# Eight value tiles of differential attention made in pairs with the gates, and two leading tiles in the last projection

## The chip, the cores and the metric

One core of a Trainium2 chip. The metric is the device time of one execution in microseconds (us); lower is better. Times before and after are medians of several runs, and one execution of each kernel was profiled.

## The reference

A two-layer trunk for 512 latent tokens and 128 context tokens (640 rows, width 2048), all in float32. Both layers: RMSNorm with a shift and a scale computed from the conditioning vector, one wide input projection whose columns are split between mixers, an output projection, and a gated residual. The second ("odd") layer, which the change is about, has differential attention (C, four heads) and grouped-query attention (D):

```
cq, ck, cv, cg, dq, dk, dv, dg = split_cols(h @ w_in, ODD_SPLIT)
...
cv = cv.reshape(b, t, C_HEADS, C_V_DIM).transpose(0, 2, 1, 3)     # 4 heads, 256 columns each
...
new = (ck, cv, k_d, v_d)                     # of the context tokens; these are outputs
cv_all = jnp.concatenate([ctx[1], cv], axis=2)      # latent tokens: cached rows, then their own
o1 = attend(cq[:, 0][:, :, None], ck_all[:, 0], cv_all)[:, :, 0]
o2 = attend(cq[:, 1][:, :, None], ck_all[:, 1], cv_all)[:, :, 0]
o_c = rms_norm(o1 - lam * o2, c_on) * (1.0 - lam_init)
y_c = o_c.transpose(0, 2, 1, 3).reshape(b, t, C_W) * jax.nn.silu(cg)
y_d = merge_heads(attend(q_d, dk_all, dv_all)) * jax.nn.silu(dg)
return jnp.concatenate([y_c, y_d], axis=-1) @ w_out, new
```

`cv`, the values of C, are 1024 columns of the projection: eight tiles of 128, two for each head. `cg` and `dg` are the gates, eight tiles each.

## The kernel before

Activations stay transposed: a tile is 128 columns of a projection on the partitions, by 640 tokens. Every float32 operand is split into a rounded part and a rest (`split`: a copy on ACT for `hi`, a subtraction on DVE for `lo`), and a product is three matmuls: hi x hi, hi x lo, lo x hi. A tile needs 16 rows of K, each in two halves of 320 tokens: 16 x 2 x 3 = 192 matmuls of 128x320, into two PSUM tiles `pa` and `pb`.

There are two ways to make tiles.

- **Singles** (`run_tiles`): a tile at a time, in four quarters (`proj_q`, four rows of K in each half: 24 + 24 matmuls). Weights come as `raw` by SP's queue, quarters ahead, and are split into `wh`, `wl` (four buffers each). After every quarter `slot` advances other work: `prep` holds what follows a tile (`q_gen`, `k_gen`, `v_gen`), `attn` holds attention (`pair_gen` for D, `diff_gen` for C, one step a call), and `fill` is a generator that is called at a given rate. With `steps` above 1 attention gets more than one step a quarter.
- **Pairs** (`run_pairs`, called at the end of `project`): two tiles by two halves of the tokens by two halves of K in seven products of 24 matmuls (`pq`) instead of eight, with sums of weights and of inputs made on DVE beside them. Results arrive as four halves of 320 tokens by `done`.

A projection begins with leading tiles, made side by side as the rows of `h` become ready; the third of them takes the PSUM tile `Sp`, which shares its two banks with attention's scores `S`.

The order of the stages around the change is:

1. Front of the odd layer (the `project` call at line 1430, jobs `FRONT`): 14 of the 16 gate tiles, three leading, three single, eight in four pairs. `gate_out` makes silu's two instructions for each half and stores the tile in `gdram`.
2. The odd run (`run_tiles` at line 1484) with 38 tiles: 12 for D, six for each C head (`q0 q1 k0 k1 v0 v1`), and at last the gates 4 and 5 (`very_late_gate`). `k_gen` norms and rotates a key in four quarters and calls `drain(attn)` before it overwrites keys; `v_gen` stages a value tile, transposes it to rows, splits it, and after the second value tile of a head appends the head's attention. The fill of this run, `fill1`, makes the last four column blocks of the second layer's modulation on DVE (`ada_on_dve`): for each block 32 loads `adaw` of 128 KB by SP's queue into three buffers, two multiply-adds of 128x256 on DVE for each (lines 211 and 213), then a sum over partitions on PE (`T<-acc,ones`, line 219), a copy on ACT and a transpose. A block is 33 calls; the rate is `FILL1 = 1.0` a quarter after the first 16 quarters (`FILL1_FROM`).
3. The last projection (`project_out(1, ...)`, order of K quarters 0, 2, 3, 1): `y1_maker(k)` loads row tile k of the mixers' output from `ydram` (`yin`) and splits it into `h`. At k = 12 it finishes `fill1` and attention, closes the pool `odd`, opens `fin`, and starts the `forms` for the pairs. Three tiles lead, three are single, ten are in five pairs.

```
    brisk = {len(jobs), len(jobs) + 1}
    ...
    run_tiles(jobs, I["od_w_in"][0], None, fill1, FILL1, fill_from=FILL1_FROM,
              steps=lambda i: 1.5 if i in brisk else 1.0)
    drain(prep)
    drain(attn)

    def y1_maker(k):
        if k == 12:
            for _ in fill1:
                pass
            drain(attn)
```

Tile (the layer under the kernel) puts each engine's instructions into a fixed order at build time and sets the semaphores; engines work through their lists in that order, and so does SP with its DMA issues.

Of the kernel before, what the change touches and what calls it, by code (L numbers as in the profile page):

```python
# [11 lines left out]
F32 = mybir.dt.float32  # L12
F32R = mybir.dt.float32r
# [7 lines left out]
P = 128  # L21
# [32 lines left out]
def trunk_kernel(ctx: ExitStack, tc: tile.TileContext, I: dict, O: dict):  # L54
# [520 lines left out]
                                   op0=ALU.add, op1=ALU.mult)  # L575


    def k_gen(ap, pp, tag, src, gain, new_out):
        raw = ap.tile([P, 2, P], F32, tag="ctxk", name="ctxk", bufs=1)
        nc.sync.dma_start(raw, src.rearrange("(c p) d -> p c d", p=P))  # L580
        x = stage(ap, pp)
        yield
        ss = small.tile([P, 5], F32, tag="ss", name="ss")
        kg = ap.tile([P, 5, P], F32, tag="rp", name="kg", bufs=3)
        junk = ap.tile([P, P * st["sets"]], F32, tag="junk", name="junk", bufs=1)[:, 0:P]
        for sample in (True, False):
            t = to_rows(cols_of(x), sample)
            for i, b in enumerate(range(4) if sample else (4,)):
                A.activation(junk, t[:, i * P:(i + 1) * P], AF.Square, accum_out=ss[:, b:b + 1])
            if sample:  # L590
                V.tensor_mul(kg[:, 0:4, :], t.rearrange("p (b f) -> p b f", b=4),
                             gain[:, None, :].to_broadcast([P, 4, P]))
            else:
                V.tensor_mul(kg[:, 4, :], t, gain)
        r = small.tile([P, 5], F32, tag="r", name="r")
        V.tensor_scalar(ss, ss, 1.0 / P, EPS, ALU.mult, ALU.add)
        G.tensor_tensor(r, ss, half[:, 0:5], op=ALU.pow)
        V.tensor_mul(kg, kg, r[:, :, None].to_broadcast([P, 5, P]))
# [12 lines left out]
        yield  # L611
        drain(attn)
        hi, lo = (ap.tile([P, 896], F32R, tag=tag + t, name=tag + t) for t in "hl")
        st[tag] = (hi, lo)
        t = psT()
        for c in range(2):
            PE.transpose(t[:, c * P:(c + 1) * P], raw[:, c, :], ident)
        split(hi[:, 0:CTX], lo[:, 0:CTX], t[:, 0:CTX])
        t = to_rows(lambda b: m1[:, b, :], True)
        split(hi[:, CTX:CTX + NS], lo[:, CTX:CTX + NS], t)  # L620
        t = to_rows(lambda b: kg[:, b, :], False)
        split(hi[:, CTX + NS:CTX + NT], lo[:, CTX + NS:CTX + NT], t)


    def q_gen(ap, pp, tag, gain, then=None, wait=True):
# [46 lines left out]
    def v_gen(ap, pp, src, new_out, w=P, j=0, then=None):  # L672
        x = stage(ap, pp)
        yield
        if j == 0:
            drain(attn)
            st["v"] = tuple(ap.tile([P, 7, w], F32R, tag=t, name=t) for t in ("vh", "vl"))
            ctx_v(ap, src, *st["v"], w)
        hi, lo = st["v"]
        cols = slice(j * P, (j + 1) * P)  # L680
        t = to_rows(cols_of(x), True)
        split(hi[:, 2:6, cols], lo[:, 2:6, cols], t.rearrange("p (b f) -> p b f", b=4))
# [3 lines left out]
        split(hi[:, 6, cols], lo[:, 6, cols], vp)  # L686
        nc.gpsimd.dma_start(new_out, vp)
        if then:
            attn.append(then())
# [141 lines left out]
    xdram, hdram, gdram = ([dram.tile([P, NT], F32, name=f"{n}{k}") for k in range(KT)] for n in ("xd", "hd", "gd"))  # L831

    y = [None] * KT
    st = {"sets": 1}
# [89 lines left out]
        open_pool("even")  # L924


    def k_job(tag, src, gain, new_out):
        return lambda pp: k_gen(pools["cur"], pp, tag, src, gains[gain], new_out)

    def v_job(src, new_out, *a):  # L930
        return lambda pp: v_gen(pools["cur"], pp, src, new_out, *a)
# [179 lines left out]
    def form_of(i):  # L1111
        return lambda j: (T[j][:, 0, i * HALF:(i + 1) * HALF], T[j][:, 1, i * HALF:(i + 1) * HALF])

    def project(w, cols, n0, maker, job, begin, part, done, tail, **kw):

        go_on = run_tiles([(cols[n], job(n)) for n in range(3)], w, maker, **{"order": (0, 2, 1, 3), **kw})


        quarters = [(cols[n], qd) for n in range(3, n0) for qd in range(4)]
# [10 lines left out]
        for n in range(3, n0):  # L1130
            pp, t = new_pp((n - 3) % 2), 4 * (n - 3)
# [270 lines left out]

    half_done, outs = set(), {}

    def front_job(n):
        def f(pp):
            put = gate_out(n)
# [11 lines left out]
    def front_tail(name):  # L1419

        if name == "P6":
# [8 lines left out]
    project(I["od_w_in"][0], [(OD["cg"] + i * P) if i < 8 else OD["dg"] + (i - 8) * P for i in FRONT], N_FRONT, h1_maker,  # L1430
            front_job, front_begin, None, front_done, front_tail, by_half=True)
    nc.sync.dma_start(tables, I["k_tables"])
    close("mid")
# [28 lines left out]
    for n in range(4):  # L1462
# [3 lines left out]
        jobs.append((OD["dq"] + (h + 1) * P, q_job("q1", "d_q_norm", then if n % 2 else None)))  # L1466
        if n % 2 == 0:
            jobs.append((OD["dk"] + kv * P, k_job(f"k{kv}", I["cache_d_k"][0, 0, kv], "d_k_norm", O["new_d_k"][0, 0, kv])))
            jobs.append((OD["dv"] + kv * P, v_job(I["cache_d_v"][0, 0, kv], O["new_d_v"][0, 0, kv], P, 0, then)))
    for h in range(4):  # L1470
        for m in range(2):
            jobs.append((OD["cq"] + (m * 4 + h) * P, q_job(f"q{m}", "c_q_norm")))
        for m in range(2):
            jobs.append((OD["ck"] + (m * 4 + h) * P,
                         k_job(f"k{m}", I["cache_c_k"][0, 0, m, h], "c_k_norm", O["new_c_k"][0, 0, m, h])))
        for j in range(2):
            jobs.append((OD["cv"] + h * 256 + j * P,
                         v_job(I["cache_c_v"][0, 0, h], O["new_c_v"][0, 0, h][:, j * P:(j + 1) * P], 256, j,
                               diff_then(h) if j else None)))
# [4 lines left out]
    run_tiles(jobs, I["od_w_in"][0], None, fill1, FILL1, fill_from=FILL1_FROM,  # L1484
              steps=lambda i: 1.5 if i in brisk else 1.0)
    drain(prep)
    drain(attn)


    def y1_maker(k):  # L1490
# [95 lines left out]
```

## Time and profile before

| | |
|---|---|
| median of 3 runs | 2317.5 us (2316.15 to 2321.3) |
| profiled execution | 2318.59 us, span 2316.8 us |
| mean granted TensorE clock | 0.997 |
| PE matmul busy | 2272.1 us (98%) |
| DVE, ACT, POOL busy | 1635.5, 969.7, 175.6 us |
| memory read, written | 301.93 MB, 38.28 MB |

The span is the time from the first to the last instruction; what lies around it is the difference to the execution's own time. PE is TensorE's matmul row, PEld its weight loads, DVE VectorE, ACT ScalarE, POOL GpSimd, SP the engine that issues most DMAs. In the groups the numbers are the sum of busy time, the mean of one instruction in ns, and the idle time of the engine ahead of them with what ended it. Matmuls are pipelined and their recorded durations overlap.

### The profile page before, as it was taken

To read this page: it belongs to the slowest core of one execution; us is meant where nothing else is said; L and a number is where in the kernel's file an instruction comes from. 1 tells how busy PE (TensorE), PEld (TensorE's weight loads), DVE (VectorE), ACT (ScalarE), POOL (GpSimd) and SP (SyncE) were. 2 spreads that over 40 slices of the span, in tenths; PEclk is the share of its full clock that TensorE was granted. 3 is DMA by queue.
4 is the path that set the end of the run, shared out by engine and by line. 5 is a ranking of instruction groups with operands and counts; after the bars stand their busy time and mean duration, and the time that the engine had idled before them with its cause. 6 is when DMAs were issued, how large, how long until landed. Compare 5 with 4: busy or idle time off the path is not lost.

```text
span 2316.8 us, 41604 instructions
## 1 busy us (share of the span) xinstructions
PE 2272.1 (98%) x15892; PEld 2197.3 (95%) x15892; DVE 1635.5 (71%) x3308; ACT 969.7 (42%) x2007; POOL 175.6 (8%) x243
## 2 busy tenths in 40 slices
PE   7999999999999999999999999999999999999999
PEld 5699999999999999999999999999999999999999
DVE  4559886786866663988887658659657658557576
ACT  4335442433422222544644445555453444434343
POOL 2111000000000000000100000000001010100101
PEclk9999999999999999999999999999999999999999
DMA  9874545445455543844773433224315233318532
GB/s 364 330 260 130 154 124 163 144 122 165 121 180 160 152 139 114 283 140 127 242 223 107 135 102 97 63 81 131 97 52 153 66 92 113 92 60 281 176 119 70
DMA packets 388456, 342.94 MB, mean 148 GB/s; under 512 B 19298, under 2 KB 327024, under 8 KB 387744
## 3 DMA queue, kind: packets, MB, share of 16 engines
q1 hardware_dynamic: 376000, 294.35, 41.9%
q0 software_dynamic: 11536, 43.77, 5.0%
q8 instruction: 125, 2.05, 0.4%
q10 hardware_dynamic: 720, 2.16, 0.3%
q14 instruction: 75, 0.61, 0.1%
HBM read 301.93 MB, written 38.28 MB: 147 GB/s over the span
## 4 chain that ended last, share of the span: by engine, by line
PE 86%; DVE 4%; ACT 3%; DMA 3%; issue 2%; POOL 1%; SPq 0%; ACTq 0%; POOLq 0%; DVEq 0%
PE pa L276 9%; PE pb L277 9%; PE pb L276 9%; PE pa L277 9%; PE pb L278 9%; PE pa L278 9%; PE pq L535 5%; PE pq L537 5%; PE pq L536 5%; PE T L715 2%; PE T L178 1%; PE S L727 1%; PE S L729 1%; PE S L728 1%; DMA yin<-yd 1%
## 5 line engine op out<-in xcount | busy, mean ns | idle before, releaser
L241 ACT ACTIVATE wh<-raw 128x512 fp32r<-128x512 f32 (+1 forms) x466 | 288.4, 619 | 723.8 <-PE pb L277 615.4
L276 PE MATMUL pa<-h,wh 128*128 128x320 f32 x1632 | 519.2, 319 | 4.8 <-ACT h L908 2.5
L242 DVE TENSOR_TENSOR wl<-raw,wh 128x512 fp32r<-128x512 f32 (+1 forms) x466 | 313.8, 674 | 296.3 <-ACT wh L241 260.9
L277 PE MATMUL pa<-h,wh 128*128 128x320 f32 x1632 | 508.3, 312 | 2.8 <-DVE h L242 2.7
L278 PE MATMUL pa<-h,wl 128*128 128x320 f32 x1632 | 506.9, 311 | 0.0
L278 PE MATMUL pb<-h,wl 128*128 128x320 f32 x1632 | 505.5, 310 | 0.0
L276 PE MATMUL pb<-h,wh 128*128 128x320 f32 x1632 | 505.2, 310 | 0.0
L277 PE MATMUL pb<-h,wh 128*128 128x320 f32 x1632 | 505.0, 309 | 0.0
L213 DVE SCALAR_TENSOR_TENSOR acc<-adaw,sT,acc 128x512 f32<-128x512 f32 (+1 forms) x600 | 358.3, 636 | 14.0 <-DMA adaw<-in_ada_w 13.7
L276 PEld LDWEIGHTS pa<-h,wh 128*128 128x128 f32 x1632 | 307.9, 189 | 18.2 <-issue 9.3
L277 PEld LDWEIGHTS pa<-h,wh 128*128 128x128 f32 x1632 | 308.4, 189 | 7.3 <-DVE h L242 4.5
L278 PEld LDWEIGHTS pa<-h,wl 128*128 128x128 f32 x1632 | 307.9, 189 | 3.3 <-issue 3.3
L278 PEld LDWEIGHTS pb<-h,wl 128*128 128x128 f32 x1632 | 306.6, 188 | 2.1 <-issue 2.1
L276 PEld LDWEIGHTS pb<-h,wh 128*128 128x128 f32 x1632 | 306.7, 188 | 0.0
L277 PEld LDWEIGHTS pb<-h,wh 128*128 128x128 f32 x1632 | 306.5, 188 | 0.1
L535 PE MATMUL pq<-h,wh 128*128 128x320 f32 x480 | 149.7, 312 | 0.4 <-DVE xr L1099 0.2
L536 PE MATMUL pq<-h,wh 128*128 128x320 f32 x480 | 148.4, 309 | 0.0
L537 PE MATMUL pq<-h,wl 128*128 128x320 f32 x480 | 148.0, 309 | 0.0
L701 ACT ACTIVATE p<-S,nm,rq 128x768 f32<-128x768 f32 (+3 forms) x120 | 101.2, 843 | 101.4 <-DVE nm L696 67.1
L535 PE MATMUL pq<-T,wh 128*128 128x320 f32 x360 | 111.2, 309 | 0.0
L536 PE MATMUL pq<-T,wh 128*128 128x320 f32 x360 | 111.2, 309 | 0.0
L537 PE MATMUL pq<-T,wl 128*128 128x320 f32 x360 | 111.2, 309 | 0.0
(326 smaller groups left out, 3699.8 us busy)
## 6 DMA issues: line engine op xcount, KB each, us to landing
adaw<-in_ada_w SPq DMA_DIRECT2D x192, 256.0 KB, 3.0
raw<-in_ev_w_in SPq DMA_DIRECT2D x184, 256.0 KB, 3.0
raw<-in_od_w_in SPq DMA_DIRECT2D x184, 256.0 KB, 2.9
ada<-in_ada_w SPq DMA_DIRECT2D x14, 2048.0 KB, 10.5
adaw<-in_ada_w SPq DMA_DIRECT2D x128, 128.0 KB, 2.2
yd<-y POOLq DMA_DIRECT2D x32, 320.0 KB, 3.0
yin<-yd SPq DMA_DIRECT2D x32, 320.0 KB, 4.4
w<-yd SPq DMA_DIRECT2D x32, 320.0 KB, 4.1
```

Of the source, the lines that this page charges most:

```text
L178: PE.matmul(acc[32 * g:32 * g + 32, 0:wd], sT[:, kt, :], w[:, kt % m, :], start=(i < 4), stop=(i >= KT - 4), tile_position=(0, 32 * g))
L213: V.scalar_tensor_tensor(out=a, in0=w, scalar=sT[:, kt, c:c + 1], in1=a, op0=ALU.mult, op1=ALU.add)
L241: A.activation(hi, x, AF.Copy)
L242: V.tensor_sub(lo, x, hi)
L276: PE.matmul(ps, wh[:, i, :], hi[:, sl], start=(j == js[0] if alone else (pos == 0 and j == 0)), stop=False)
L277: PE.matmul(ps, wh[:, i, :], lo[:, sl], start=False, stop=False)
L278: PE.matmul(ps, wl[:, i, :], hi[:, sl], start=False, stop=(j == js[1] - 1 if alone else (pos == 3 and j == 3)))
L535: PE.matmul(ps, wh[:, j, :], hi, start=(h == 0 and j == 0), stop=False)
L536: PE.matmul(ps, wh[:, j, :], lo, start=False, stop=False)
L537: PE.matmul(ps, wl[:, j, :], hi, start=False, stop=(h == 1 and j == 3))
L701: A.activation(p[:, 0:n], s, AF.Exp, scale=rsc, bias=nm, accum_out=l)
L715: PE.transpose(t[:, i * P:(i + 1) * P], p, ident)
```

## The change

The eight value tiles of C leave the odd run and join the front as four more pairs behind the gates'. `value_out` copies each half to SBUF; when a tile is whole, `value_rows` transposes it to rows of tokens, stores it in `vdram` (128x640), and writes the context part to the output. In the odd run the first key tile of a C head (`k0`) now also loads the head's two value tiles back (`vx`, in the buffers `stg`), and splits them with the cached values; the second key tile (`k1`) appends the head's attention. The odd run has 30 tiles instead of 38; from tile 13 on attention gets 1.1 steps a quarter, and 1.5 in the two last gates as before. The last projection has two leading tiles instead of three, hence four single ones; attention is no longer drained at the end of the odd run but runs on beside the first two units of the leading tiles, which leave `S` free. So `y1_maker` takes its first eight rows into the buffers `rp` and `stg` instead of `P`, which attention still uses.

```diff
-    def k_gen(ap, pp, tag, src, gain, new_out):
+    def k_gen(ap, pp, tag, src, gain, new_out, vals=None, then=None):
+        vx = []
+        def v_in(j):
+            vx.append(ap.tile([P, 5, P], F32, tag="stg", name="vx", bufs=2))
+            nc.sync.dma_start(vx[j].rearrange("p b f -> p (b f)"), vals[1][j])
...
         x = stage(ap, pp)
+        if vals:
+            v_in(0)
         yield
...
+        if vals:
+            v_in(1)
...
+        if vals:
+            yield
+            hi, lo = st["v"] = tuple(ap.tile([P, 7, 2 * P], F32R, tag=t, name=t) for t in ("vh", "vl"))
+            ctx_v(ap, vals[0], hi, lo, 2 * P)
+            for j in range(2):
+                cols = slice(j * P, (j + 1) * P)
+                split(hi[:, 2:7, cols], lo[:, 2:7, cols], vx[j])
+        if then:
+            attn.append(then())
...
-    def project(w, cols, n0, maker, job, begin, part, done, tail, **kw):
+    def project(w, cols, n0, maker, job, begin, part, done, tail, n_lead=3, **kw):
...
+    def value_rows(n, t):
+        yield
+        r = pools["cur"].tile([P, 5, P], F32, tag="xr", name="vr", bufs=3)
+        A.copy(r[:, 0:4, :], to_rows(cols_of(st[t]), True).rearrange("p (b f) -> p b f", b=4))
+        A.copy(r[:, 4, :], to_rows(cols_of(st[t]), False))
+        nc.gpsimd.dma_start(vdram[n], r.rearrange("p b f -> p (b f)"))
+        nc.gpsimd.dma_start(O["new_c_v"][0, 0, n // 2][:, n % 2 * P:(n % 2 + 1) * P], r[:, 4, :])
+
+    def value_out(n):
+        def put(t, sl, src):
+            A.copy(st[t][:, sl], src)
+            if (n, "v") in half_done:
+                prep.append(value_rows(n, t))
+            half_done.add((n, "v"))
+        return put
...
-            outs[t] = gate_out(N_FRONT + 2 * p + t)
+            n = N_FRONT + 2 * p + t
+            outs[t] = gate_out(n) if n < len(FRONT) else value_out(n - len(FRONT))
...
-    project(I["od_w_in"][0], [...cg and dg of FRONT...], N_FRONT, h1_maker,
+    project(I["od_w_in"][0], [...cg and dg of FRONT...]
+            + [OD["cv"] + i * P for i in range(8)], N_FRONT, h1_maker,
...
         for m in range(2):
+            more = (None, diff_then(h)) if m else ((I["cache_c_v"][0, 0, h], vdram[2 * h:2 * h + 2]),)
             jobs.append((OD["ck"] + (m * 4 + h) * P,
-                         k_job(f"k{m}", ..., O["new_c_k"][0, 0, m, h])))
-        for j in range(2):
-            jobs.append((OD["cv"] + h * 256 + j * P, v_job(...)))
+                         k_job(f"k{m}", ..., O["new_c_k"][0, 0, m, h], *more)))
 
-    brisk = {len(jobs), len(jobs) + 1}
+    brisk = {len(jobs): 1.5, len(jobs) + 1: 1.5}
+    brisk.update((i, 1.1) for i in range(13, len(jobs)))
...
     drain(prep)
-    drain(attn)
...
-            t = pools["cur"].tile([P, 768], F32, tag="P", name="yin", bufs=P_BUFS)[:, 0:NT]
+            tag, n = (("rp", 3), ("stg", 2))[k % 2]
+            t = pools["cur"].tile([P, NT], F32, tag=tag, name="yin", bufs=n)
...
-    project_out(1, y1_maker, rows_out, rows_last, lambda name: None, order=(0, 2, 3, 1))
+    project_out(1, y1_maker, rows_out, rows_last, lambda name: None, n_lead=2, order=(0, 2, 3, 1))
```

More of the change, by code (lines that the diff above doesn't have):

```diff
@@ L670, in ctx_v, with v_gen @@
         split(hi[:, 0:2, :], lo[:, 0:2, :], raw)
-    def v_gen(ap, pp, src, new_out, w=P, j=0, then=None):
+    def v_gen(ap, pp, src, new_out, then=None):
         x = stage(ap, pp)
         yield
-        if j == 0:
-            drain(attn)
[L677 to L680, printed above, removed]
+        drain(attn)
+        hi, lo = st["v"] = tuple(ap.tile([P, 7, P], F32R, tag=t, name=t) for t in ("vh", "vl"))
+        ctx_v(ap, src, hi, lo, P)
         t = to_rows(cols_of(x), True)
-        split(hi[:, 2:6, cols], lo[:, 2:6, cols], t.rearrange("p (b f) -> p b f", b=4))
+        split(hi[:, 2:6, :], lo[:, 2:6, :], t.rearrange("p (b f) -> p b f", b=4))
         t = to_rows(cols_of(x), False)
@@ L685, in v_gen @@
         V.tensor_copy(vp, t)
-        split(hi[:, 6, cols], lo[:, 6, cols], vp)
+        split(hi[:, 6, :], lo[:, 6, :], vp)
         nc.gpsimd.dma_start(new_out, vp)
@@ L830, in trunk_kernel @@
     x0dram = [dram.tile([P, 4 * NT + 1], F32, name=f"x0d{g}") for g in range(4)]
-    xdram, hdram, gdram = ([dram.tile([P, NT], F32, name=f"{n}{k}") for k in range(KT)] for n in ("xd", "hd", "gd"))
+    xdram, hdram, gdram, vdram = ([dram.tile([P, NT], F32, name=f"{n}{k}") for k in range(KT)]
+                                  for n in ("xd", "hd", "gd", "vd"))
     y = [None] * KT
@@ L924, in even_start, with k_job @@
         open_pool("even")
-    def k_job(tag, src, gain, new_out):
-        return lambda pp: k_gen(pools["cur"], pp, tag, src, gains[gain], new_out)
+    def k_job(tag, src, gain, new_out, *a):
+        return lambda pp: k_gen(pools["cur"], pp, tag, src, gains[gain], new_out, *a)
     def v_job(src, new_out, *a):
@@ L1112, in form_of @@
         return lambda j: (T[j][:, 0, i * HALF:(i + 1) * HALF], T[j][:, 1, i * HALF:(i + 1) * HALF])
-    def project(w, cols, n0, maker, job, begin, part, done, tail, **kw):
-        go_on = run_tiles([(cols[n], job(n)) for n in range(3)], w, maker, **{"order": (0, 2, 1, 3), **kw})
-        quarters = [(cols[n], qd) for n in range(3, n0) for qd in range(4)]
+    def project(w, cols, n0, maker, job, begin, part, done, tail, n_lead=3, **kw):
+        go_on = run_tiles([(cols[n], job(n)) for n in range(n_lead)], w, maker, **{"order": (0, 2, 1, 3), **kw})
+        quarters = [(cols[n], qd) for n in range(n_lead, n0) for qd in range(4)]
         raws, parts = [], []
@@ L1129, in project @@
         go_on()
-        for n in range(3, n0):
-            pp, t = new_pp((n - 3) % 2), 4 * (n - 3)
+        for n in range(n_lead, n0):
+            pp, t = new_pp((n - n_lead) % 2), 4 * (n - n_lead)
             for hv in ([HV] if n < n0 - 1 else [HV[1:], HV[:1]]):
@@ L1428, in front_tail @@
                     split(hi[:, HALF:NT], lo[:, HALF:NT], t[:, i * HALF:(i + 1) * HALF])
-    project(I["od_w_in"][0], [(OD["cg"] + i * P) if i < 8 else OD["dg"] + (i - 8) * P for i in FRONT], N_FRONT, h1_maker,
+    project(I["od_w_in"][0], [(OD["cg"] + i * P) if i < 8 else OD["dg"] + (i - 8) * P for i in FRONT]
+            + [OD["cv"] + i * P for i in range(8)], N_FRONT, h1_maker,
             front_job, front_begin, None, front_done, front_tail, by_half=True)
@@ L1468, in trunk_kernel @@
             jobs.append((OD["dk"] + kv * P, k_job(f"k{kv}", I["cache_d_k"][0, 0, kv], "d_k_norm", O["new_d_k"][0, 0, kv])))
-            jobs.append((OD["dv"] + kv * P, v_job(I["cache_d_v"][0, 0, kv], O["new_d_v"][0, 0, kv], P, 0, then)))
+            jobs.append((OD["dv"] + kv * P, v_job(I["cache_d_v"][0, 0, kv], O["new_d_v"][0, 0, kv], then)))
     for h in range(4):
@@ L1473, in trunk_kernel @@
         for m in range(2):
+            more = (None, diff_then(h)) if m else ((I["cache_c_v"][0, 0, h], vdram[2 * h:2 * h + 2]),)
             jobs.append((OD["ck"] + (m * 4 + h) * P,
-                         k_job(f"k{m}", I["cache_c_k"][0, 0, m, h], "c_k_norm", O["new_c_k"][0, 0, m, h])))
-        for j in range(2):
-            jobs.append((OD["cv"] + h * 256 + j * P,
-                         v_job(I["cache_c_v"][0, 0, h], O["new_c_v"][0, 0, h][:, j * P:(j + 1) * P], 256, j,
-                               diff_then(h) if j else None)))
-    brisk = {len(jobs), len(jobs) + 1}
+                         k_job(f"k{m}", I["cache_c_k"][0, 0, m, h], "c_k_norm", O["new_c_k"][0, 0, m, h], *more)))
+    brisk = {len(jobs): 1.5, len(jobs) + 1: 1.5}
+    brisk.update((i, 1.1) for i in range(13, len(jobs)))
     for i in (4, 5):
@@ L1484, in trunk_kernel @@
     run_tiles(jobs, I["od_w_in"][0], None, fill1, FILL1, fill_from=FILL1_FROM,
-              steps=lambda i: 1.5 if i in brisk else 1.0)
+              steps=lambda i: brisk.get(i, 1.0))
     drain(prep)
-    drain(attn)
     def y1_maker(k):
```

## The prediction

> **What bounds the kernel now.** I began with the page's busy times and the windows view (busy time of each engine in a stretch of the span), then went to the groups by line with shapes kept apart, the chain of waits and the timeline.
>
> ```profile
> PE 2272.1 (98%) x15892; PEld 2197.3 (95%) x15892; DVE 1635.5 (71%) x3308; ACT 969.7 (42%) x2007; POOL 175.6 (8%) x243
> ```
>
> ```profile
> core 0: us, PE busy (x) PEld busy (x) DVE busy (x) ACT busy (x) POOL busy (x), PEclk, DMA share, GB/s
> 1180.00:1320.00 140.00, 140.00 (x955) 139.80 (x954) 104.28 (x176) 64.26 (x115) 5.94 (x11) 1.00 0.44 135
> ...
> 1666.00:2090.00 424.00, 415.24 (x2895) 403.46 (x2893) 272.62 (x629) 187.56 (x444) 40.81 (x52) 1.00 0.31 92
> ...
> 2090.26:2137.30 47.04, 44.40 (x293) 42.98 (x294) 37.63 (x66) 22.81 (x36) 2.77 (x4) 1.00 0.88 283
> 2106.00:2128.00 22.00, 20.15 (x133) 19.27 (x131) 18.14 (x30) 11.49 (x17) 0.00 (x0) 1.00 0.91 296
> ```
>
> PE bounds it everywhere. The first row is the stretch of the gate pairs: it has no idle time, and 140.00 us over 955 instructions give 146.6 ns from one 128x320 matmul to the next (the recorded 310 ns overlap). The second row is the projection and attention of the differential heads: 8.8 us idle of 424. The third is the leading part of the last projection (three tiles, 288 matmuls or 42.2 us, in 47.04 us with 2.64 us idle). So a change pays by removing matmuls, and loses by any wait on PE that the order of instructions makes.
>
> **Part 1: fewer matmuls.** A pair takes seven products of 24 matmuls, 168, where two single tiles take 192. Four pairs save 96 matmuls, and 96 x 146.6 ns = 14.1 us, all on the path. In the instruction lists of both programs the PE counts differ by just these 96: the transposes of the values are as many as before (40 move to the front), and the third leading tile of the last projection comes back as a single one. Four more pairs should run as the 1180-1320 row does; a value tile has four ACT copies and no DVE work where a gate has two instructions on each, and ACT is busy for 64.26 of the row's 140 us.
>
> What the pairs cost elsewhere hides: eight stores of 320 KB and eight loads of 320 KB (POOL's and SP's queues) lie far apart in time, and the splits of the values move from PSUM to SBUF sources of about the same size. Cover gone, an SP load of this size costs 4.4 us once (the load row below), and weight loads queue behind it; I count nothing, as the weights are loaded several quarters ahead.
>
> **Part 2: the modulation fill runs late.** This decides. The last four column blocks of the second layer's modulation are made on DVE by a generator that is advanced once a quarter tile, from the 17th quarter of this run on: 33 steps a block, 132 in all. Before, the run had 38 tiles, 152 quarters, hence 136 advances: it just fitted. Now it has 30 tiles, 120 quarters, 104 advances; 28 are left, and `y1_maker` takes them all at tile row 12 of the last projection. The rate `FILL1` is unchanged. The lists show what the scheduler makes of that. In before no fill instruction follows the first `h<-yin` split of the last projection; in the changed program 40 do (20 steps of two). PE's list there reads:
>
> ```
> pb<-h11 (second lead, second unit, its last matmul)
> T<-ident,on x2
> T<-acc0,ones x2
> T<-acc1,ones x2
> T<-ident,ada_sb2 x2
> pa<-h12
> ```
>
> `T<-acc,ones` sums the finished block, so PE, which works in order, can't begin the third unit before the fill's last step. On DVE, 14 of the 20 steps stand behind the `wl` split whose buffer (four slots) PE frees only with that last matmul of the second unit. Those 14 steps therefore lie bare behind PE's work; nothing is left on PE to cover them. What a step costs:
>
> ```profile
> L213 DVE SCALAR_TENSOR_TENSOR acc<-adaw,sT,acc 128x256 f32<-128x256 f32 x240 | 103.5, 476 | 5.5 <-DMA adaw<-in_ada_w 5.3
> ...
> L242 DVE TENSOR_TENSOR wl<-raw,wh 128x512 fp32r<-128x512 f32 x442 | 304.0, 688 | 284.2 <-ACT wh L241 249.0 <-PE T L564 25.2 <-DMA raw<-in_ev_w_in 7.0
> ...
> L242 DVE TENSOR_TENSOR T<-sx,T 128x960 fp32r<-128x960 f32 x24 | 27.7, 1156 | 8.2 <-ACT T L241 7.9
> ...
> L1084 DVE TENSOR_TENSOR sx<-w,sx 128x320 f32<-128x320 f32 x24 | 11.6, 485 | 0.2
> ```
>
> ```profile
> L241 ACT ACTIVATE wh<-raw 128x512 fp32r<-128x512 f32 (+1 forms) x466 | 288.4, 619 | 723.8 <-PE pb L277 615.4
> ```
>
> ```profile
> 1915.58 2.46 DVE L213 SCALAR_TENSOR_TENSOR acc<-adaw,sT,acc 128x256 f32<-128x256 f32 x6 [0.27 <-DMA adaw<-in_ada_w]
> 1918.14 0.69 DVE L242 TENSOR_TENSOR wl<-raw,wh 128x512 fp32r<-128x512 f32 x1
> 1919.10 2.46 DVE L213 SCALAR_TENSOR_TENSOR acc<-adaw,sT,acc 128x256 f32<-128x256 f32 x6 [0.27 <-DMA adaw<-in_ada_w]
> 1921.66 0.69 DVE L242 TENSOR_TENSOR wl<-raw,wh 128x512 fp32r<-128x512 f32 x1
> 1922.75 1.67 DVE L213 SCALAR_TENSOR_TENSOR acc<-adaw,sT,acc 128x256 f32<-128x256 f32 x4 [0.40 <-DMA adaw<-in_ada_w]
> ```
>
> Three buffers hold the loaded weights: three steps take 2.46 us on DVE, and the next three start 3.52 us after the first (1915.58, 1919.10), each time ended by the DMA. So 14 steps take four groups at 3.52 and two steps: the last begin at 14.1 and end at 15.7 us. Behind them on SP's queue stand the loads of the rows 12 to 15, which before were issued long ahead:
>
> ```profile
> adaw<-in_ada_w SPq DMA_DIRECT2D x128, 128.0 KB, 2.2
> ...
> yin<-yd SPq DMA_DIRECT2D x32, 320.0 KB, 4.4
> ```
>
> ```profile
> 2101.45 4.87 DMA yin<-yd
> 2106.34 0.75 ACT h L241
> 2107.11 0.84 DVE h L242
> 2107.97 3.45 DMA yin<-yd
> ...
> 2117.89 6.05 DMA yin<-yd
> 2123.97 0.75 ACT h L241
> ...
> 2127.23 0.83 DVE h L242
> ```
>
> The last fill load goes out when the 11th step ends (four slots of the count: 10.6 + 1.6 = 12.2 us), the row's load about 0.8 later. It lands after 3.45 (chain) to 4.4 us (median); I take 3.9. ACT's split adds 0.75, so PE restarts at 13.0 + 3.9 + 0.75 = 17.6, and with the weight split ahead of the 14 steps (0.62 on ACT, 0.69 on DVE) PE stands **18.9 us**. Lower end: DVE's own pace of 2.46/3 a step (the 11th ends at 9.0) and the fast load: 9.0 + 0.8 + 3.45 + 0.75 + 1.3 = 15.3. Upper: a load of 5.2 us, between the chain's two longer ones: 20.2. I take the load pace, since the rows nearest to it are load-paced.
>
> A granted clock row bears on the restart:
>
> ```profile
> 1128.00:1132.00 4.00, 4.00 (x17) 4.00 (x17) 2.32 (x7) 3.04 (x8) 0.00 (x0) 0.50 0.66 218
> 1132.00:1136.00 4.00, 4.00 (x25) 4.00 (x25) 3.12 (x9) 3.93 (x12) 1.92 (x4) 0.87 0.43 178
> ```
>
> After PE's short stand between 1124 and 1128 us the clock was 0.50 for 4 us and 0.87 for the next 4: 2.0 + 0.5 = 2.5 us of work lost. Before, the last projection had no such stand (1.00 in its rows); now it has one. The Trainium skill (TensorE: Matmul & The Clock Gate, Part 1: The HAM clock gate) says that PE's clock falls to half after an idle window of about 3.4 us and needs as long a busy one to return. By that rule the sum would have 1.7 us here, by the row 2.5.
>
> **Part 3: after the restart, and before it.** From the split of row 12 to that of row 7 the chain above took 2106.34 to 2128.06, 21.7 us, of loads in three slots, splits and the pair forms, while PE had three leads, 144 matmuls or 21.1 us, and idled 1.85. With two leads PE has 14.1 us. The chain loses one of three forms (1.16 for `T` and four instructions like L1084's at 0.485, 3.1 us on DVE) and three weight splits (2.1): 16.5. PE idles between 2.4 and 7.6, less the 1.85 of before: 0.5 to 5.7. I take 2.5 with the cold clock in it, as slow matmuls fall into the waits. In the first two units the rows now come through five slots (three `rp`, two `stg`) instead of four own ones, some freed only by the last gate, while attention's last blocks share the engines: 0 to 3, I take 1.
>
> **Part 4: the heads.** Each differential head has four tiles instead of six.
>
> ```profile
> 1801.00:1900.00 99.00, 97.39 (x684) 95.12 (x684) 56.48 (x126) 46.82 (x113) 12.22 (x14) 1.00 0.22 66
> ...
> 1903.00:1961.00 58.00, 56.80 (x398) 55.11 (x397) 52.37 (x129) 25.64 (x54) 4.32 (x5) 1.00 0.45 131
> ```
>
> A head without fill took 99 us, DVE 56.5 of them. Two tiles less make 99 - 192 x 0.1466 = 70.9 us, and DVE 56.5 - 8 x 0.69 = 51: fine. In the head with a fill block DVE gets 33 x 0.82 = 27 more, 78 against 70.9. Splits run three quarters ahead, and at 52.37 of 58 us DVE cost PE 1.2 us, so I take 1.5 (from -2, waits gone with the value tiles, to +7, the whole excess).
>
> **The sum.** -14.1 + 18.9 + 2.5 + 1 + 1.5 = +9.8. The profiled run took 2318.59 us with a span of 2316.8 and lies 1.1 us over the median of the three runs, 2317.5; the difference is applied to the median: **2327 us**. Ends: -14.1 + 15.3 + 0.5 + 0 - 2 = -0.3, and -14.1 + 20.2 + 5.7 + 3 + 7 = +21.8.
>
> **Rivals.** 0.2% is 4.6 us, about what a measurement of this kernel can tell from no change.
>
> - *The late fill goes at DVE's pace* (0.16). In that part no weights of a tile are loaded, so the three buffers may refill sooner than at 1915 us. Then all low ends hold: 2317 us, the same. Against it: landing takes 2.2 us even in the median, and two steps cover 1.6.
> - *The fill is hidden, and the saving arrives whole* (0.10). PE's wait for `T<-acc,ones` would have to be under 4 us, which is so if three or fewer steps are left at that point (three are loaded already). Then 2317.5 - 14.1 + 2.5 + 1 = 2307 us, faster. For it: the full-speed pairs. Against it: the list, 14 steps. It decides from a stand of about 9 us downward.
> - *DVE bounds the heads* (0.08). The excess of 7 us comes out in the fill's head and some on each other, where attention now has fewer matmuls beside it: 2334 us or more.
>
> The forecast has 0.66. Slower by over 0.2%: 0.66 + 0.08 = 0.74; within: 0.16; faster: 0.10. The range takes in the second case and the terms' upper ends short of their sum: 2315 to 2337.
>
> **What would show it.** In the changed profile: the stretch of pairs longer by about 98.6 us (4 x 168 x 0.1467) at full PE; a PE gap of 15 to 20 us ahead of `T<-acc,ones` in the last projection's lead, with DVE's L213 rows in threes 3.5 us apart in it, then a clock of about 0.5; and PE idle of the heads near 9 us. I am wrong if that gap is under 9 us, if the pairs idle, or if the heads idle by over 20 us.

## The result, and the profile after

| | before | after |
|---|---|---|
| median | 2317.5 us (2314.68 to 2321.3) | 2329.76 us (2327.2 to 2334.25) |
| after / before | | 1.0056, 95% interval 1.0039 to 1.0074 |
| profiled execution | 2318.59 us, span 2316.8 | 2327.2 us, span 2325.4 |

The changed kernel is slower by 12.3 us by the medians and by 8.6 us in the two profiled executions. The prediction was 2327 us.

The page of the changed kernel, busy times:

```profile
PE 2258.1 (97%) x15796; PEld 2179.4 (94%) x15796; DVE 1678.3 (72%) x3364; ACT 990.7 (43%) x2043; POOL 181.8 (8%) x251
```

TensorE has the 96 matmuls less and 14.0 us less busy time, so 22.6 us of new waiting stand against them. (A tile is 16 x 2 x 3 = 96 matmuls, 24 in each quarter; the 192, and the 24 + 24, that are given with the kernel before are those of two tiles.) The windows view of the changed kernel (columns as in the prediction: engine busy times and counts, then the granted clock, the DMA share and GB/s) shows where:

```profile
1180.00:1320.00 140.00, 140.00 (x955) 139.80 (x954) 105.52 (x173) 62.25 (x110) 5.94 (x11) 1.00 0.43 136
1150.00:1420.00 270.00, 269.78 (x1847) 269.16 (x1847) 198.97 (x327) 130.96 (x240) 18.82 (x35) 1.00 0.45 140
...
1764.00:2083.00 319.00, 307.18 (x2141) 294.11 (x2140) 236.62 (x553) 163.97 (x396) 40.70 (x46) 1.00 0.33 101
2083.00:2135.00 52.00, 30.67 (x181) 26.91 (x182) 41.83 (x89) 14.76 (x24) 2.81 (x5) 0.80 0.71 227
2104.00:2108.00 4.00, 0.00 (x0) 0.00 (x0) 3.26 (x9) 0.00 (x0) 0.00 (x0) 0.50 0.59 178
2108.00:2112.00 4.00, 3.36 (x12) 1.52 (x12) 1.66 (x6) 2.02 (x4) 0.00 (x0) 0.50 0.86 310
2112.00:2116.00 4.00, 4.00 (x19) 4.00 (x20) 3.40 (x7) 1.42 (x3) 0.00 (x0) 0.65 0.82 264
```

The first row is as full as before, but it ends about where the gates' pairs end; the second also holds the four new pairs, which run from about 1315 to 1414, and has 0.22 us idle. The differential heads (1764 to 2083; since attention now runs on beside it, the first part of the last projection's lead lies in there too) idle for 11.8 us, where they idled for 8.8 us of 424 before. The row from 2083 on, which begins within the lead, idles for 21.3 us of 52, and its clock is 0.80. PE's timeline names what ended the largest gap (in brackets, the idle time before the row and its releaser), and DVE's shows what ran in it:

```profile
2108.03 1.46 PE L219 MATMUL T<-acc,ones 128*32 128x256 f32 x6 [17.30 <-DVE acc L213]
2121.68 0.42 PE L276 MATMUL pa<-h,wh 128*128 128x320 f32 x1 [1.62 <-ACT h L241]
```

```profile
2091.84 2.46 DVE L213 SCALAR_TENSOR_TENSOR acc<-adaw,sT,acc 128x256 f32<-128x256 f32 x6
2097.07 2.46 DVE L213 SCALAR_TENSOR_TENSOR acc<-adaw,sT,acc 128x256 f32<-128x256 f32 x6 [2.76 <-DMA adaw<-in_ada_w]
2100.13 2.58 DVE L213 SCALAR_TENSOR_TENSOR acc<-adaw,sT,acc 128x256 f32<-128x256 f32 x6 [0.60 <-DMA adaw<-in_ada_w]
2103.29 2.59 DVE L213 SCALAR_TENSOR_TENSOR acc<-adaw,sT,acc 128x256 f32<-128x256 f32 x6 [0.57 <-DMA adaw<-in_ada_w]
2106.32 0.88 DVE L213 SCALAR_TENSOR_TENSOR acc<-adaw,sT,acc 128x256 f32<-128x256 f32 x2 [0.45 <-DMA adaw<-in_ada_w]
2107.49 0.88 DVE L213 SCALAR_TENSOR_TENSOR acc<-adaw,sT,acc 128x256 f32<-128x256 f32 x2 [0.29 <-DMA adaw<-in_ada_w]
```

This is the late fill: 28 instructions, 14 steps, in 16.5 us. They come in threes; the second three starts 5.2 us behind the first, the next two 3.1 us apart, and all but the first wait for their loads.

### The profile page after: what moved, and what is told of

Same layout as the page of the kernel before. It is cut to its first block, busy times and chain, and to the rows that moved or that the text cites. A ratio compares the mean times of both kernels' runs of the same rounds, so it can differ in the third digit from the quotient of the medians.

```text
span 2325.4 us, 41522 instructions
## 1 busy us (share of the span) xinstructions
PE 2258.1 (97%) x15796; PEld 2179.4 (94%) x15796; DVE 1678.3 (72%) x3364; ACT 990.7 (43%) x2043; POOL 181.8 (8%) x251
## 4 chain that ended last, share of the span: by engine, by line
PE 85%; DVE 5%; DMA 4%; ACT 3%; issue 2%; POOL 1%; SPq 0%; POOLq 0%; ACTq 0%; DVEq 0%
PE pa L276 9%; PE pb L277 8%; PE pb L276 8%; PE pb L278 8%; PE pa L277 8%; PE pa L278 8%; PE pq L535 7%; PE pq L537 7%; PE pq L536 7%; PE T L732 2%; PE T L178 1%; DMA adaw<-in_ada_w 1%; DMA yin<-yd 1%; PE S L744 1%; PE S L745 1%
## 5 line engine op out<-in xcount | busy, mean ns | idle before, releaser
L276 PE MATMUL pa<-h,wh 128*128 128x320 f32 x1520 | 483.6, 319 | 7.5 <-ACT h L241 5.0
L277 PE MATMUL pa<-h,wh 128*128 128x320 f32 x1520 | 473.1, 312 | 1.6 <-DVE h L242 1.4
L278 PE MATMUL pa<-h,wl 128*128 128x320 f32 x1520 | 472.0, 311 | 0.0
L278 PE MATMUL pb<-h,wl 128*128 128x320 f32 x1520 | 471.3, 310 | 0.0
L277 PE MATMUL pb<-h,wh 128*128 128x320 f32 x1520 | 470.8, 310 | 0.0
L276 PE MATMUL pb<-h,wh 128*128 128x320 f32 x1520 | 470.6, 310 | 0.0
L276 PEld LDWEIGHTS pa<-h,wh 128*128 128x128 f32 x1520 | 286.4, 189 | 21.4 <-issue 8.9
L277 PEld LDWEIGHTS pa<-h,wh 128*128 128x128 f32 x1520 | 286.6, 189 | 7.0 <-DVE h L242 3.9
L276 PEld LDWEIGHTS pb<-h,wh 128*128 128x128 f32 x1520 | 285.9, 188 | 0.0
L277 PEld LDWEIGHTS pb<-h,wh 128*128 128x128 f32 x1520 | 285.7, 188 | 0.1
L535 PE MATMUL pq<-h,wh 128*128 128x320 f32 x608 | 189.7, 312 | 0.7 <-ACT wh L241 0.7
L536 PE MATMUL pq<-h,wh 128*128 128x320 f32 x608 | 187.9, 309 | 0.0
L537 PE MATMUL pq<-h,wl 128*128 128x320 f32 x608 | 187.7, 309 | 0.0
L535 PE MATMUL pq<-T,wh 128*128 128x320 f32 x456 | 140.9, 309 | 0.0
L536 PE MATMUL pq<-T,wh 128*128 128x320 f32 x456 | 140.9, 309 | 0.0
L537 PE MATMUL pq<-T,wl 128*128 128x320 f32 x456 | 140.9, 309 | 0.0
```

The costliest lines, as they stand in the source:

```text
L276: PE.matmul(ps, wh[:, i, :], hi[:, sl], start=(j == js[0] if alone else (pos == 0 and j == 0)), stop=False)
L277: PE.matmul(ps, wh[:, i, :], lo[:, sl], start=False, stop=False)
L278: PE.matmul(ps, wl[:, i, :], hi[:, sl], start=False, stop=(j == js[1] - 1 if alone else (pos == 3 and j == 3)))
L535: PE.matmul(ps, wh[:, j, :], hi, start=(h == 0 and j == 0), stop=False)
L536: PE.matmul(ps, wh[:, j, :], lo, start=False, stop=False)
L537: PE.matmul(ps, wl[:, j, :], hi, start=False, stop=(h == 1 and j == 3))
```

## The experiments

All times are medians. Each kernel is compared with the kernel before run beside it on the same chip; the difference column is to that one. Runs 1, 7 and 8 are not told apart from the kernel before: their intervals include 1.

| run | kernel | us | difference | ratio, 95% interval |
|---|---|---|---|---|
| 1 | after, fill rate 1.3 | 2319.47 | +1.9 | 1.0008 (0.9999 to 1.0016) |
| 2 | before, fill rate 0.765 | 2327.12 | +9.5 | 1.0039 (1.0026 to 1.0051) |
| 3 | before, two leads | 2324.50 | +6.9 | 1.0034 (1.0022 to 1.0046) |
| 4 | after, fill 1.12 from the first quarter | 2325.89 | +8.3 | 1.0038 (1.0025 to 1.0051) |
| 5 | pairs alone, fill 1.3 | 2312.27 | -4.9 | 0.9973 (0.9964 to 0.9982) |
| 6 | pairs alone, fill late | 2322.46 | +5.3 | 1.0017 (1.0008 to 1.0025) |
| 7 | run 5, two leads | 2319.16 | +2.0 | 1.0008 (0.9998 to 1.0017) |
| 8 | run 1, rows 12 to 15 on GpSimd's queue | 2315.28 | -1.9 | 0.9993 (0.9985 to 1.0002) |
| 9 | run 5, attention faster at the end | 2306.17 | -11.1 | 0.9954 (0.9942 to 0.9966) |
| 10 | run 9, fill spread | 2313.30 | -4.0 | 0.9985 (0.9976 to 0.9993) |
| 11 | run 1, attention faster at the end | 2310.69 | -7.0 | 0.9974 (0.9965 to 0.9983) |
| 12 | after, attention faster at the end | 2330.75 | +12.9 | 1.0054 (1.0040 to 1.0068) |

The first theory was the prediction's: the loss is the late fill. The rivals were the heads and the two leads. A "stand" below is a stretch in which PE waits.

### Run 1: the fill in time

```diff
-FILL1 = 1.0
+FILL1 = 1.3
```

> The changed kernel with the rate of the modulation fill raised from 1.0 to 1.3 advances a quarter tile, so that all 132 steps are taken within the run of the heads and none is left to the last projection. Theory (late fill): the 17.6 us stand of TensorE ahead of the sum of the finished block goes, with the half clock behind it (about 2 us) and part of the short waits of the rows 12 to 15; the heads take 0 to 3 us more, because their two blocks of the fill now lie in fewer quarters. Time 2306 to 2313 us; no gap over 2 us between the second and third unit of the lead; clock 1.00 there. Rival (the heads have no room): DVE is full in the two heads with a fill block, TensorE idles there by 8 us or more beyond the 22 us of the changed kernel, and the time stays at 2318 or above. Rival (two leads are too few): the rows' loads and splits set the lead anyway, the stand turns into waits of 10 us or more at the h splits, and the time stays above 2320.

2319.47 us: 10.4 us are gained against after (in differences to before), less than the stand and its clock. The time lies above the theory's 2306 to 2313 us and just short of the 2320 us of the rival of the two leads. The heads are not it: from 1764 to 2060 PE idles for 9.3 us, against 10.3 us in after. PE's timeline of this run has another gap at the same place, with another releaser, and the chain of waits shows what led to it:

```profile
2103.32 0.64 PE L276 MATMUL pa<-h,wh 128*128 128x320 f32 x1 [8.27 <-ACT h L241]
```

```profile
2094.83 0.23 PE T L1386 x2
...
2095.09 0.04 DVE y L1391
2095.12 0.31 issue
2095.43 0.69 DVE wl L242
...
2096.14 0.37 SPq L254
...
2096.60 5.91 DMA yin<-yd
...
2102.53 0.74 ACT h L241
```

PE's first piece is the last transpose of attention's last head (L1386). A weight split on DVE, a weight load on SP and then the load of row 12 all come behind it; the row lands and is split 8 us later. So under the fill lay a second wait.

### Runs 2 and 3: the kernel before with one part each

Run 2, then run 3:

```diff
-FILL1 = 1.0
+FILL1 = 0.765
```

```diff
-    project_out(1, y1_maker, rows_out, rows_last, lambda name: None, order=(0, 2, 3, 1))
+    project_out(1, y1_maker, rows_out, rows_last, lambda name: None, n_lead=2, order=(0, 2, 3, 1))
```

> The kernel before with the rate of the fill lowered from 1.0 to 0.765, so that the same 28 advances are left to row 12 of the last projection, with no pair and no lead changed. Theory (late fill alone makes the loss): a stand of TensorE ahead of the sum of the finished block and rows 12 to 15 loaded late. With three leads in the lead part more weight splits stand open ahead of the fill on DVE, and only 4 of the 26 late instructions lie behind the last split, so the stand is 4 to 12 us instead of 17.6, and the time 2322 to 2331 us. Rival (the loss comes from the pairs, the heads or the two leads): the stand is under 3 us and the time stays within 3 us of the kernel before.

> The kernel before with two leading tiles instead of three in the last projection, and nothing else: the third tile comes back as a single one, so TensorE has the same matmuls. Theory: 48 matmuls (7.0 us) fewer lie beside the chain of loads, splits and pair forms in the lead, which itself loses one of three forms and three weight splits (5.2 us); TensorE idles 0.5 to 5.7 us more there, 2.5 as the value taken, so 2318 to 2323 us with 2320 as the value. Rival (two leads do not cover the chain at all): 7 us or more, 2324 and above. Rival (the loads set it and the shorter chain is gained): within 1 us of the kernel before.

Each makes a loss without any pair: +9.5 us for the late fill, within its range (its profiled execution was the shortest of its runs, 2320.96 us, with a stand of only 2.2 us, so the loss is not read from that trace), and +6.9 us for two leads, above the 2318 to 2323 us expected. In run 3 no gap is long, but the rows come one by one (PE's timeline):

```profile
2111.95 0.41 PE L276 MATMUL pa<-h,wh 128*128 128x320 f32 x1 [1.68 <-ACT h L241]
2116.10 0.41 PE L276 MATMUL pa<-h,wh 128*128 128x320 f32 x1 [1.25 <-ACT h L241]
2117.98 0.41 PE L277 MATMUL pa<-h,wh 128*128 128x320 f32 x1 [1.03 <-DVE h L242]
```

Two leads leave these loads and splits uncovered.

### Run 4: the fill earlier

```diff
-FILL1 = 1.0
-FILL1_FROM = 16
+FILL1 = 1.12
+FILL1_FROM = 0
```

> The changed kernel with the fill at 1.12 advances a quarter from the first quarter of the run on, instead of 1.0 from the 17th: the same 132 steps end within the run, at a lower rate, and the eight tiles of the dense heads carry more of them. Theory (late fill): as with the rate of 1.3, the stand goes; the heads are loaded more evenly, so 2304 to 2312 us and 0 to 3 us less than with 1.3. Rival (the dense heads have no room): TensorE idles more in the first four tiles than is gained later, and it takes 2 us or more longer than with 1.3.

6.4 us longer than run 1: the rival. The stand at row 12 is there as in run 1 (8.63 us). In the dense heads (D's, 1412 to 1666) DVE is busy for 185.61 us against 177.44 in run 1, and PE for 250.37 against 252.08, at a clock of 0.99 against 1.00. But in the differential heads (1764 to 2060) PE is busy for less too, 284.32 us against 286.74, though DVE has less to do there, 220.95 us against 232.67. So a fuller DVE in the dense heads is a part of the loss only.

### Runs 5 and 6: the pairs without the lead's changes

Run 5 against after; run 6 is the same with `FILL1 = 1.0`:

```diff
-FILL1 = 1.0
+FILL1 = 1.3
...
     drain(prep)
+    drain(attn)
...
-            tag, n = (("rp", 3), ("stg", 2))[k % 2]
-            t = pools["cur"].tile([P, NT], F32, tag=tag, name="yin", bufs=n)
+            t = pools["cur"].tile([P, 768], F32, tag="P", name="yin", bufs=P_BUFS)[:, 0:NT]
...
-    ... n_lead=2, order=(0, 2, 3, 1))
+    ... n_lead=3, order=(0, 2, 3, 1))
```

> The changed kernel with the rate 1.3, and with the last projection's lead as in the kernel before: three leading tiles, attention finished ahead of them, rows 0 to 3 and 8 to 11 through the four wide buffers P. What is left of the change is the four more pairs and the value rows in DRAM. Theory (the loss lies in the lead, in two parts: the late fill and the lead's own changes): 96 matmuls or 14.1 us saved, 2.3 us given back in the heads (TensorE's idle time of 10.5 us there with the rate 1.3 against 8.2 before), the lead as before: 2304 to 2309 us. Rival (the pairs or the heads cost more than their idle time shows): 2312 us or above.

> As the kernel before this one (pairs alone, the lead as before), but with the fill's rate at 1.0, so that 28 advances are left to row 12. Theory: the late fill costs here about what it cost the kernel before at the lowered rate (9.5 us by the medians), less than the 17.6 us stand of the changed kernel, since a third leading tile gives TensorE work beside it: 2311 to 2319 us. Rival (the stand is the same whatever the lead): 2321 us or above. Rival (three leads hide it): within 3 us of the kernel with the rate 1.3.

The pairs alone pay, but 4.9 us instead of the 8 to 13 expected. Run 6 lies above its 2311 to 2319 us, in the range of the rival that the stand is as long with any lead, though the stand is not. The late fill costs 10.2 us here (+5.3 less -4.9), about the same as between run 1 and after, with a short gap: PE's timeline of run 6, and its clock behind the gap:

```profile
2111.95 1.46 PE L219 MATMUL T<-acc,ones 128*32 128x256 f32 x6 [3.39 <-DVE acc L213]
```

```profile
2112.00:2116.00 4.00, 3.39 (x12) 1.56 (x13) 1.43 (x5) 1.26 (x3) 0.00 (x0) 0.50 0.99 350
2116.00:2120.00 4.00, 3.77 (x13) 3.21 (x14) 3.25 (x6) 1.96 (x3) 0.00 (x0) 0.50 0.85 295
```

At least 3.6 us go in these 8 us to the half clock (half of the busy 7.16). In run 5 the missing microseconds are at the end of the heads:

```profile
2076.30 0.69 PE L1386 MATMUL T<-ident,on 128*128 128x128 f32 x2 [2.18 <-DVE on L1380]
2085.57 0.66 PE L1386 MATMUL T<-ident,on 128*128 128x128 f32 x2 [2.69 <-DVE on L1380]
```

By the code, the last head's attention is now ready only at the end of a key's preparation, which takes more quarters than a value tile's did, and the 1.5 steps in each of the last eight quarters no longer finish it. Its last pieces stand behind both gate tiles, where before they were spread among them, so they run without a tile's matmuls beside them: PE's timeline has no `pa` or `pb` row from 2074 to 2086.

### Runs 7 and 8: what made row 12 late

Run 7 is run 5 with `n_lead=2`. Run 8 is run 1 with the loads of rows 12 to 15 on another queue:

```diff
-        nc.sync.dma_start(t, ydram[k])
+        (nc.gpsimd if k >= 12 and st["late"] else nc.sync).dma_start(t, ydram[k])
```

(`st["late"]` is set ahead of the last projection.)

> The changed kernel with the rate 1.3, two leading tiles, but attention finished ahead of them and the rows through the buffers P; SyncE's queue then has one weight load ahead of row 12 instead of four. Theory (of the 8.3 us stand with the rate 1.3, the place of row 12's load on that queue is the cause): no gap over 3 us in the lead, and only the price of two leads is left, 6.9 us by the kernel before with two leads: 2311 to 2316 us. Rival (two leads make the stand whatever the queue): a gap of 6 us or more ahead of the third unit and 2317 us or above. Rival (the third lead is worth nothing here): as the pairs alone, 2304 to 2309 us.

> The changed kernel with the rate 1.3, and rows 12 to 15 and 4 to 7 as they were except that the loads of rows 12 to 15 in the last projection are issued by GpSimd's queue instead of SyncE's. Theory (row 12's load stood behind four weight loads, the last of which waits for a buffer that comes free at the end of the second unit): the load goes out 5 us or more before the second unit ends, the 8.3 us gap shrinks to 3 us or less, the cold clock behind it (3.1 us) goes, and the time is 2309 to 2314 us. Rival (the load waits for something else, such as the memory that attention's last block still holds): the gap stays at 6 to 9 us and the time within 2 us of 2319.5.

Run 7 has no such stand, but costs 6.9 us over run 5, as two leads did in run 3; that is more than the 2311 to 2316 us expected, and its runs spread from 2313.0 to 2326.3 us. Run 8 gains 3.8 us, more than its rival allowed, yet its gap is still there as that rival had it; what it gained lies elsewhere, in part behind the gap, where run 1 had a wait of 1.20 us at 2114.99 that run 8 has not. So leaving SP's queue does not bring row 12 early. GpSimd's row shows why:

```profile
2101.60 0.64 PE L276 MATMUL pa<-h,wh 128*128 128x320 f32 x1 [8.52 <-ACT h L241]
```

```profile
2093.84 1.12 POOL L856 DMA_DIRECT2D yd<-y  x2 [2.47 <-DVE y L1391]
2095.01 1.66 POOL L1122 DMA_DIRECT2D yin<-yd  x3
```

The loads go out right behind the stores of attention's last output, which wait for its last block. On either queue row 12 comes behind the end of attention. Whether it is the order or the memory that attention's buffers hold until then, these runs don't tell.

### Runs 9 to 12: attention's end

One line, put into run 5 (run 9), run 1 (run 11) and after (run 12):

```diff
-    brisk = {len(jobs): 1.5, len(jobs) + 1: 1.5}
+    brisk = {len(jobs): 2.0, len(jobs) + 1: 2.0}
```

Run 10 is run 9 with `FILL1 = 1.2` and `FILL1_FROM = 8`.

> The pairs alone (rate 1.3, lead as before), with attention advanced by 2.0 instead of 1.5 steps a quarter in the last two tiles of the heads. Theory (of the 14.1 us saved about 3.6 are given back at the end of the heads, where the last head's attention starts later than before and its two waits of 2.2 and 2.7 us ahead of the transposes of its outputs lie bare): these waits go below 1 us each and the time falls by 2 to 4 us, to 2308 to 2310.5 us. Rival (the waits only move into the two tiles): within 1 us of 2312.3.

> As the kernel before this one, with the fill at 1.2 advances a quarter from the 9th quarter on, instead of 1.3 from the 17th. Theory (DVE's load in the heads with a fill block costs TensorE 1 to 3 us): another 0 to 2 us less than the kernel with the rate 1.3. Rival (an early fill meets the dense heads, where DVE is fuller, as with the rate 1.12 from the first quarter, which took 6.4 us longer than 1.3): 2 us or more longer.

> The changed kernel with its two leads, buffers and late drain of attention, the fill's rate at 1.3 and attention at 2.0 steps a quarter in the last two tiles of the heads. Theory (with the rate 1.3 the 8.3 us stand ahead of row 12 hung on attention's last block, which lay in the second unit of the lead): attention ends before the lead, the stand shrinks to 3 us or less with no cold clock behind it, and the price of two leads alone is left, 6.9 us over the 2306.2 of three leads: 2311 to 2315 us. Rival (two leads cannot cover row 12's load, whatever attention does): a gap of 5 us or more stays there and the time is 2316 us or above. Rival (two leads are as good as three once attention is out of the way): 2304 to 2309 us.

> The changed kernel with one edit: attention at 2.0 steps a quarter in the last two tiles of the heads; the fill stays at 1.0 and hence late. Theory (the two waits lie one over the other: the stand of 17.3 us ahead of the third unit covers the 8.3 us wait behind attention's last block, so the late fill's 10.3 us are only what it sticks out): taking the one away while the other stays gains 0 to 4 us, 2326 to 2330 us, with the stand still at 15 to 18 us. Rival (the two add up): the gain is the 8.8 us that it was with the rate 1.3, so 2319 to 2322 us, and the stand is 10 us or less.

Run 9 is the fastest kernel: 6.2 us less than run 5, more than the 2 to 4 expected, and 11.1 us less than before. From 2083 on its lead again runs almost full, at the full clock (a wait of 1.92 us stands at its beginning, at 2077.06):

```profile
2083.00:2135.00 52.00, 50.21 (x342) 49.34 (x342) 40.68 (x73) 24.40 (x39) 4.28 (x7) 1.00 0.88 290
```

Run 11 gains 8.9 us over run 1, and its stand falls from 8.27 us to this:

```profile
2103.92 0.42 PE L276 MATMUL pa<-h,wh 128*128 128x320 f32 x1 [2.87 <-ACT h L241]
```

So the second wait was attention's late end. What is left of it still costs the clock, which is 0.57 from 2104 to 2108. In run 12 the same edit gains nothing (+12.9 against +12.3), and the stand of the fill is still there:

```profile
2113.77 1.46 PE L219 MATMUL T<-acc,ones 128*32 128x256 f32 x6 [15.81 <-DVE acc L213]
```

The two waits lie one over the other, as the theory had it, with the time just above its 2326 to 2330 us. Put as differences to before:

| two leads | attention 2.0 | attention 1.5 |
|---|---|---|
| fill in time | -7.0 | +1.9 |
| fill late | +12.9 | +12.3 |

With attention out of the way the late fill costs 19.9 us; with attention late it costs 10.4, since 8.9 are lost anyway.

Run 10 was a miss, 7.1 us longer than run 9. Part of it is seen where the fill now meets the dense heads; the windows of run 9 and of run 10:

```profile
1440.00:1500.00 60.00, 59.87 (x415) 58.97 (x414) 35.80 (x78) 28.42 (x61) 4.22 (x5) 1.00 0.32 95
```

```profile
1440.00:1500.00 60.00, 58.61 (x405) 57.44 (x404) 50.54 (x117) 27.01 (x60) 4.94 (x5) 1.00 0.45 131
```

DVE goes from 35.80 to 50.54 us of 60, and PE loses 1.3. The larger part is lost in the differential heads: from 1764 to 2060 PE is busy for 281.70 us in run 10 and for 286.92 in run 9, at a clock of 0.99 against 1.00, though DVE has less to do there (226.04 us against 233.97). Why PE waits more there, these runs don't tell.

## Why the prediction was right

**The pairs (part 1).** They run at full PE, as forecast. The stretch is longer by 99.6 us (forecast 98.6), read from the first load of a differential head's cached keys; before, then after (behind the durations stand the first and the last start). The first load of D's cached keys, which is nearer to the pairs, moves by 97.8 us:

```profile
L580 SPq DMA_DIRECT2D ctxk<-in_cache_c_k x8: 368/388/486, 1512.3 to 2002.2; - x8
```

```profile
L587 SPq DMA_DIRECT2D ctxk<-in_cache_c_k x8: 367/368/956, 1611.9 to 2015.7; - x8
```

Run 9, which has the pairs and, in the lead, only the new wait of 1.92 us, measures this part with the heads: -11.1 us (-13.4 to -7.9 by the interval), against -14.1 + 1.5 = -12.6. The kernel before was not run with attention at 2.0; from 2040 to 2090 its PE has no wait over 0.54 us, so little was to be had there.

**The late fill (part 2).** The stand came where the instruction lists put it. From 2090.73, where PE's gap begins, to the first matmul of the third unit, at 2110.59 in PE's timeline, it is 19.9 us, 2.2 of them the block's own sums and transposes; forecast 18.9. Its price with nothing under it is also 19.9 us (run 12 less run 11, each known to within 2 to 3 us). Two details were off. The loads came 3.1 us apart and not 3.52, but the second group waited 2.76 us for its load. And row 12's load did not end the stand: SP and ACT of after, in that order:

```profile
2092.75 12.63 SPq L207 DMA_DIRECT2D adaw<-in_ada_w  x11
2105.43 1.37 SPq L1122 DMA_DIRECT2D yin<-yd  x3
```

```profile
2109.53 0.37 ACT L222 COPY ada_sb<-T 128x256 f32<-128x256 f32 x1 [19.05 <-PE T L219]
2109.80 1.37 ACT L241 ACTIVATE h<-yin 128x640 fp32r<-128x640 f32 x2
```

The row goes out behind the eleven fill loads, as predicted, and lands 3.9 us later, at 2109.3, as predicted too; but ACT comes to it only at 2109.80, since it stood behind the copy of the block's sum. The step "the last fill load, the row's load, ACT's split" should have ended at the sum and the copy, by a margin of 0.5 us.

**The clock.** By the working of the prediction's row, half of 3.36 and 0.35 of 4.00, the restart lost 1.7 + 1.4 = 3.1 us; forecast 2.5. Of the 3.1, 1.0 lies in the block's own sums and transposes (2.09 us busy at half clock from 2108.00 to 2110.59), which the 19.9 contains already. The estimate from the rule of the Trainium skill (TensorE: Matmul & The Clock Gate, Part 1: The HAM clock gate) was 1.7; the measurement decides.

**After the restart and before it (part 3).** Two leads, with the late drain of attention and the buffers that came with them, cost 4.1 us (run 11 less run 9), against 2.5 + 1 = 3.5. In the kernel before they cost 6.9, beyond the upper end of 5.7. What the step "attention's last blocks share the engines: 0 to 3, I take 1" missed is attention's late end, 8.9 us (run 1 less run 11). It is not in the result only because the fill's stand covers it (run 12), and that is luck: the prediction had neither the wait nor the cover.

**The heads (part 4).** 11.8 us of idle time where "near 9" was forecast, under the 20 that would have refuted it. They don't bound, but DVE is nearer to it than its 236.6 of 319 us say: with a fill block, from 1851 to 1922, it is busy for 66.57 of 71 us, where the prediction had 78 against 70.9, and PE idles there for 3.7 us.

**The sum.** Measured by the runs: -11.1 + 4.1 + 19.9 = +12.9 with attention's end taken away (differences from run 9 to 11 to 12, so they add up of themselves), and +12.3 as it is, of which attention's end is 8.9 and the fill then only 10.4; forecast +9.8. The three rivals fall: the fill's groups follow its loads, not DVE's pace; the gap is 17.3 us and not under 9; the heads have room. But "the saving arrives whole" is near what run 9 shows (2306.17 us, with three leads, where that rival had 2307), when fill and attention are set to the shorter run.

## What to carry to other kernels

When work moves out of a loop, whatever is advanced once per turn of that loop (here a fill and attention's steps) is left over at its end: count the turns against the steps needed, and set the rates anew. Removing the wait that a trace names shows the next one below it, so the price of a wait is known only with the waits that it covers taken away too: of two edits of one line each, one alone gained 10.4 us, the other nothing, and both together 19.3 us. A leading tile that seems to be in the way can be the cover for the loads behind it.

## What the runs showed of the hardware

The granted clock fell after waits much shorter than the stand. In run 5 the longest waits at the end of the heads are 2.18 us and 2.69 us, and the clock is 0.50 behind the first of them (first row). It is still 1.00 from 2074 to 2075 and 0.55 in the next microsecond, so it fell about 1 us into that wait. In run 3 three waits of 1.0 to 1.7 us follow each other (the other rows):

```profile
2076.00:2080.00 4.00, 3.29 (x14) 3.00 (x15) 2.26 (x8) 1.53 (x4) 0.00 (x0) 0.50 0.41 99
```

```profile
2116.00:2120.00 4.00, 2.87 (x13) 2.61 (x14) 3.67 (x6) 2.31 (x4) 0.00 (x0) 0.81 0.62 178
2120.00:2124.00 4.00, 4.00 (x23) 4.00 (x22) 3.63 (x8) 1.75 (x2) 0.00 (x0) 0.76 0.99 314
```

The Trainium skill (TensorE: Matmul & The Clock Gate, Part 1: The HAM clock gate) lets the clock fall after an idle window of about 3.4 us; these rows do not agree. Not each such wait costs it: in run 9 the clock is 1.00 after the wait of 1.92 us.

So short waits can cost more than their sum. From 2068 to 2135 PE is busy for 60.70 us of 67 in run 5 and for 62.39 us in run 9, which is only 1.7 us more; the clock is 0.92 in the one and 1.00 in the other. Of the 6.2 us between the two kernels the larger part is thus the clock and not the waits.
